# Attention keys and queries projected with a head's columns on the partitions, the rotary embedding made of products and shifted adding transfers

## The chip, the core and the metric

The kernel runs on one core of a Trainium2 chip. The metric is the time of one launch on the device in microseconds (us), the median of several runs. Inputs and outputs lie in device memory (DRAM); the core has a matrix engine (PE, whose weight loads the profile lists as PEld), a vector engine (DVE), a scalar engine (ACT), GpSimd (POOL) and a queue engine (SP). ACT, POOL and SP also issue transfers (DMAs).

## What is computed

One block of a model with two branches, for 256 tokens and 256 context tokens of width 2048, 16 query heads and 4 key/value heads of 128 columns. Both token sets are normalised and modulated, then multiplied by one wide matrix `w_in`; its columns are queries, keys, values and gates of a windowed attention with sinks, five groups of a gated recurrence (HGRN), and two merge gates. Only the part that the change touches is written out:

```python
def apply_axial_rope(x, cos, sin):
    x1, x2, x3, x4 = jnp.split(x, 4, axis=-1)
    rot = jnp.concatenate([-x2, x1, -x4, x3], axis=-1)
    return x * cos[:, None, :] + rot * sin[:, None, :]
q = apply_axial_rope(aq.reshape(B, n, 16, 128), cos, sin) * 128 ** -0.5
k = apply_axial_rope(ak.reshape(B, n, 4, 128), cos, sin)
k_c = cak.reshape(B, L, 4, 128)          # the context's keys are not rotated
out = sink_softmax_av(q @ concat(k_window, k_c).T, concat(v_window, v_c), sink)
```

The rotation adds to each column of a head, times a cosine, the column 32 places away (within its pair of 32-column groups), times a signed sine. The scores need queries and keys with the 128 columns of a head on the partitions and the tokens along the row.

## The kernel before, in words

Every fp32 operand is kept as a high part (rounded to the matrix engine's fp32r) and a low part (the rest). A product is three matmuls: high by high, high by low, low by high. Weights are read from DRAM in pieces of 128x1024 ("chunks", `raw`, five buffers, issued by SP far ahead); ACT rounds a chunk to `wh` (L85) and DVE subtracts it to make `wl` (L86), three buffers each, and PE multiplies.

The stages in order of time:

1. To about 132 us: norms and modulation.
2. To about 440 us: the projections with all 512 tokens and others whose result has tokens on the partitions. `quad_tok` is a Strassen-like product of seven half-size products (L732, L734, L737) with 256 columns each, used for the recurrence's values (four times), for all keys (`C_K`, 512 columns of 4 heads) and for all values (`C_V`); its results go to DRAM (`kv_dr`).
3. From about 440 to 700 us: `quad_col`, the same scheme with a head's columns on the partitions (L660 with 512 columns, L663 with 256), two heads a time, 13 sets, for the forget gates; ACT ends a set with a sigmoid and an affine step and stores it (`F_dr`).
4. From about 700 to 1256 us, the weave: eight pairs of recurrence heads. The small work of a pair (`pair`, a generator) is woven by `weave` with large projections that serve as filler (`side_work`). A filler block is 8 chunks. `proj_tok_g` gives tokens on the partitions (each chunk 12 matmuls of 512 columns: L100, L101, L103); `proj_col_x_g` gives columns on the partitions (each chunk 8 matmuls of 512 columns, L154, high weights by both halves of x, and 8 of 256, L157; two half-blocks of 4 chunks). The blocks are, two per pair: merge, queries 0; merge, gate; queries 1, merge; gates, merge; queries 2, merge; gates, merge; queries 3, merge; the rest. The gates g of the residual are made in the background by `gates`: DVE adds one 128x512 piece of `w_ada` at a time (L204, tile `hgw`), and POOL fetches the next into the same buffer (L541) when DVE is done.
5. Then attention (`attend`) with the output projections as filler, and the two last projections.

In the weave PE's order is written out by the program; DVE, ACT and POOL are ordered by a scheduler that simulates the program, and each engine runs its list strictly in that order. `behind_chunk` only forbids an instruction a place ahead of the last chunk's ACT and DVE steps.

Keys and queries before: at the end of a query block DVE rotates the two 128x512 results from the matmul banks (`rope`, four instructions, L1074 to L1082), ACT stores them (`qr_dr`, L527), and each store puts a task on a list. `tasks_on` starts tasks at fixed places of a pair (filler steps 7, 11, 15): POOL fetches the tile back (L1133), PE turns it with four transposes (`turn_tile`, L1098), ACT and DVE split it into high and low parts (L1100, L1101), and POOL stores those (`q_dr`, L1139). The four key tasks at the weave's start do the same from `kv_dr` (L1106); the tokens' keys are rotated after the fetch.

## Time and profile before

| | |
|---|---|
| median of 3 runs | 1584.49 us (1583.45 to 1588.19) |
| the profiled execution | 1586.59 us, span of its instructions 1584.8 us (1.8 us lie around it) |
| busy share of the span | PE 99%, PEld 85%, DVE 76%, ACT 54%, POOL 9% |
| granted PE clock | 0.999 |
| DMA | 333.83 MB, mean 211 GB/s |
| transfers on POOL's queue | 64.08 MB, 11.8% of 16 engines' span |

A busy PE means only that some matmul is in flight: matmuls overlap, one of 512 columns lasts about 390 ns but a new one starts every 227 to 230 ns. What a group of matmuls costs is therefore read from starts, in the order of time, not from durations. Idle time of an engine off the path costs nothing; a wait on ACT or DVE counts when it makes the next `wh` or `wl` late for PE.

### The profile page before, as it was taken

The numbers are of one execution on the slowest core, as the hardware profiler recorded it, in microseconds if no ns is written. First come the engines' busy times: TensorE is split into PE (matmuls) and PEld (weight loads), VectorE is DVE, ScalarE is ACT, GpSimd is POOL, SyncE is SP. The second block draws the span as 40 slices with busy tenths as digits, with TensorE's granted clock in tenths as the row PEclk, the third lists the DMA queues.
The fourth block names the chain that finished last, engine by engine and source line by source line (L and its number), as shares of the span: only waits on it lengthen the run. The fifth ranks groups of instructions, "written<-read, shape, count | busy, mean of one in ns | idle before, by whom it ended". The sixth has DMA issues, their size and how long they took to land. (4 is left out here: it accounts for less than half of the span.)

```text
span 1584.8 us, 27868 instructions
## 1 busy us (share of the span) xinstructions
PE 1561.6 (99%) x10954; PEld 1343.8 (85%) x10954; DVE 1201.5 (76%) x1764; ACT 860.5 (54%) x1344; POOL 142.1 (9%) x280
## 2 busy tenths in 40 slices
PE   7999999999999999999999999999999999999998
PEld 4568899999988888888888888888888888888887
DVE  4449977777787878878888897888878777757764
ACT  4336443333355555566656666575666776744442
POOL 2000000000000000011212222121121000000000
PEclk9999999999999999999999999999999999999999
DMA  9996734434444444467777877878677854458661
GB/s 366 386 387 230 226 111 130 134 132 134 133 147 127 134 130 137 136 225 252 243 247 244 300 260 233 270 243 273 221 261 249 289 159 154 155 180 295 226 197 69
DMA packets 242900, 333.83 MB, mean 211 GB/s; under 512 B 12080, under 2 KB 162000, under 8 KB 242000
## 3 DMA queue, kind: packets, MB, share of 16 engines
q1 hardware_dynamic: 214096, 249.54, 48.5%
q0 software_dynamic: 19168, 64.08, 11.8%
q10 hardware_dynamic: 9504, 18.42, 3.2%
q8 instruction: 86, 1.41, 0.4%
q14 instruction: 46, 0.38, 0.1%
HBM read 300.53 MB, written 31.47 MB: 209 GB/s over the span
## 5 line engine op out<-in xcount | busy, mean ns | idle before, releaser
L85 ACT ACTIVATE wh<-raw 128x1024 fp32r<-128x1024 f32 x284 | 298.8, 1059 | 236.3 <-PE pj L101 151.7
L86 DVE TENSOR_TENSOR wl<-raw,wh 128x1024 fp32r<-128x1024 f32 x284 | 344.0, 1219 | 89.9 <-ACT wh L85 88.9
L100 PE MATMUL pj<-wh,xHL 128*128 128x512 f32 (+1 forms) x768 | 298.6, 390 | 0.0
L101 PE MATMUL pj<-wh,xHL 128*128 128x512 f32 (+1 forms) x768 | 294.8, 385 | 0.0
L103 PE MATMUL pj<-wl,xHL 128*128 128x512 f32 (+1 forms) x768 | 202.7, 385 | 0.0
L635 ACT ACTIVATE wh<-T 128x1024 fp32r<-128x1024 f32 x75 | 79.5, 1060 | 166.8 <-DVE T L616 83.9
L100 PEld LDWEIGHTS pj<-wh,xHL 128*128 128x128 f32 x768 | 144.4, 188 | 28.2 <-ACT sg L219 0.6
L101 PEld LDWEIGHTS pj<-wh,xHL 128*128 128x128 f32 x768 | 144.5, 188 | 27.6
L103 PEld LDWEIGHTS pj<-wl,xHL 128*128 128x128 f32 x768 | 142.0, 188 | 28.9
L635 ACT ACTIVATE wh<-raw 128x1024 fp32r<-128x1024 f32 x100 | 105.3, 1055 | 71.9 <-PE pj L734 23.7
L154 PE MATMUL pj<-xHL,wh 128*128 128x512 f32 x512 | 130.3, 396 | 0.0
L636 DVE TENSOR_TENSOR wl<-raw,wh 128x1024 fp32r<-128x1024 f32 x100 | 121.8, 1218 | 9.8 <-ACT wh L635 9.7
L636 DVE TENSOR_TENSOR wl<-T,wh 128x1024 fp32r<-128x1024 f32 x75 | 91.5, 1220 | 32.8 <-ACT wh L635 32.8
L154 PEld LDWEIGHTS pj<-xHL,wh 128*128 128x128 f32 x512 | 92.4, 189 | 16.9
L157 PEld LDWEIGHTS pj<-xHL,wl 128*128 128x128 f32 x512 | 69.8, 190 | 5.2
L204 DVE SCALAR_TENSOR_TENSOR acc<-hgw,cg,acc 128x512 f32<-128x512 f32 x60 | 44.9, 748 | 35.0 <-DMA hgw<-in_w_ada_dram 35.0
L157 PE MATMUL pj<-xHL,wl 128*128 128x256 f32 x512 | 71.3, 282 | 0.0
L912 DVE TENSOR_TENSOR A<-A,X 128x512 f32<-128x512 f32 x96 | 61.6, 682 | 0.1
L616 DVE TENSOR_TENSOR T<-raw,T 128x1024 f32<-128x1024 f32 x50 | 60.9, 1218 | 0.1
L616 DVE TENSOR_TENSOR raw<-raw 128x1024 f32<-128x1024 f32 x25 | 30.6, 1225 | 36.7 <-DMA raw<-in_w_in_dram 36.7
L541 POOL DMA_DIRECT2D hgw<-in_w_ada_dram x64 | 35.0, 547 | 235.3 <-DVE acc L204 157.6
L660 PE MATMUL pj<-S,wh 128*128 128x512 f32 x208 | 52.6, 395 | 1.6 <-ACT s L667 1.6
(353 smaller groups left out, 3155.1 us busy)
## 6 DMA issues: line engine op xcount, KB each, us to landing
raw<-in_w_in_dram SPq DMA_DIRECT2D x300, 512.0 KB, 4.6
raw<-in_w_ada_dram SPq DMA_DIRECT2D x64, 512.0 KB, 8.0
hgw<-in_w_ada_dram POOLq DMA_DIRECT2D x64, 256.0 KB, 4.5
raw<-in_w_o_hgrn_dram SPq DMA_DIRECT2D x32, 512.0 KB, 3.6
raw<-in_w_o_attn_dram SPq DMA_DIRECT2D x32, 512.0 KB, 4.1
raw<-in_w_out_dram SPq DMA_DIRECT2D x28, 512.0 KB, 4.1
F<-F POOLq DMA_DIRECT2D x16, 512.0 KB, 7.2
F<-F ACTq DMA_DIRECT2D x13, 512.0 KB, 4.4
```

The costliest lines, as they stand in the source:

```text
L85: last_hi[0] = act.activation(h[:, :n], raw[:, :n], AF.Copy).ins
L86: last_lo[0] = dve.tensor_tensor(lo[:, :n], raw[:, :n], h[:, :n].bitcast(F32), op=ALU.subtract).ins
L100: pe.matmul(o, s[0], m[0], start=first, stop=False)
L101: pe.matmul(o, s[1], m[0], start=False, stop=False)
L103: pe.matmul(o, s[0], m[1], start=False, stop=last)
L154: pe.matmul(o.rearrange("p (a t) -> p a t", a=2), h[:, j, cs_], xHL[:, :, k0 + j, :T], start=k0 + j == 0, stop=False)
L157: pe.matmul(o[:, :T], lo[:, j, cs_], xH[:, k0 + j, :T], start=False, stop=k0 + j == KT - 1)
L616: dve.tensor_tensor(o, x_, y_, op=ALU.subtract)
L635: act.activation(h, src, AF.Copy)
L636: dve.tensor_tensor(lo, src, h.bitcast(F32), op=ALU.subtract)
L660: pe.matmul(m_[z].rearrange("p (z a t) -> p z a t", z=2, a=2), h[:, k, :], mv(k), start=fresh and k == 0, stop=False, skip_group_check=True)
L912: dve.tensor_tensor(av, av, f.unsqueeze(3).to_broadcast([P, 2, n2, b]), op=ALU.mult)
```

## The change

The tables of cosine and sine are turned (columns of a head on the partitions, sines moved by 32 partitions). Keys leave `quad_tok` and become two more sets of `quad_col` (`key_set`), after the first and the third forget set of stage 3; their end is four DVE products of 128x256, two ACT copies and two stores. Queries become `proj_col_x_g` blocks; a half-block ends with two ACT copies and two DVE sums (`halves_into`), two DVE products of 128x512 (`times_row`, by cosine and by sine), and two stores into separate DRAM tiles. A task now fetches the cosine product into `qx` (L1119 after the change), then adds the sine product to it by four accumulating POOL transfers of 32 partitions each, every one from the neighbouring 32 rows (L1125), and then splits with ACT and DVE (L1104, L1105 for keys, L1156, L1157 for queries). No transposes are left on this way. The context's keys are fetched and split with nothing added. `tasks_on` now does one step at a time, at filler steps 5, 7, 9, 11, 13 and 15. The layout of the loaded queries in `attend` follows.

```diff
-    kv_dr = [[dram.tile([P, 1024], F32, name=f"kv{i}_{t}") for t in range(2)] for i in range(2)]
-    qr_dr = [dram.tile([P, 1024], F32, name=f"qr{j}") for j in range(4)]
+    av_dr = [dram.tile([P, 1024], F32, name=f"av{t}") for t in range(2)]
+    k_dr = [[dram.tile([P, w], F32, name=f"k{n}_{w}") for w in (1024, 512)] for n in range(2)]
+    qr_dr = [[dram.tile([P, 1024], F32, name=f"qr{j}_{y}") for y in range(2)] for j in range(4)]
+    def times_row(o, a, c0):
+        dve.tensor_tensor(o.rearrange("p (h t) -> p h t", h=2), a.rearrange("p (h t) -> p h t", h=2),
+                          cs[:, c0: c0 + T].unsqueeze(1).to_broadcast([P, 2, T]), op=ALU.mult)
+    def halves_into(o, bank_):
+        act.activation(o, bank_[:, T:], AF.Copy)
+        dve.tensor_tensor(o, bank_[:, :T], o, op=ALU.add)
+        def key_set(n):
+            def finish(sg):
+                kc = fp.tile([P, 2, 512], F32, tag="F0", name="kc", bufs=2)
+                ks = base.tile([P, 512], F32, tag="bb", name="ks", bufs=2)
+                for i in (1, 0):
+                    for o, c0 in ((kc[:, i, :T], K_COS), (ks[:, i * T: (i + 1) * T], K_SIN)):
+                        dve.tensor_tensor(o, sg[i][:, :T], cs[:, c0: c0 + T], op=ALU.mult)
+                    act.activation(kc[:, i, T:], sg[i][:, T:], AF.Copy)
+                nc.scalar.dma_start(k_dr[n][0], kc.rearrange("p i t -> p (i t)"))
+                nc.scalar.dma_start(k_dr[n][1], ks)
+            quad_col(C_K + 2 * n * HD, finish)
-            for i, co in enumerate((C_K, C_V)):
-                quad_tok(co, kv_dr[i])
+            quad_tok(C_V, av_dr)
             for n in range(1, 8):
...
+                if n < 3:
+                    key_set(n - 1)
-        task[0] = (task[0]() if task[0] else None) or (tasks.pop(0)() if tasks else None)
+        if task[0]:
+            task[0] = task[0]()
+        elif tasks:
+            task[0] = tasks.pop(0)()
+    def rotated(src, then):
+        def fetch():
+            a = base.tile([P, 512], F32, tag="sm", name="qx", bufs=3).rearrange("p (h t) -> p h t", h=2)
+            nc.gpsimd.dma_start(a, src[0])
+            if src[1] is None:
+                return lambda: lambda: then(a)
+            def more():
+                for b in range(4):
+                    nc.gpsimd.dma_start(a[32 * b: 32 * b + 32], src[1][32 * (b ^ 1): 32 * (b ^ 1) + 32], accum_op=ALU.add)
+                return lambda: then(a)
+            return more
+        return fetch
-        bq = yield from proj_tok_g(w_in, C_Q + 512 * j, x_st, range(2))
-        for t in range(2):
-            qr = base.tile([P, 512], F32, tag="sm", name="qr", bufs=3)
-            rope(qr.rearrange("p (r h d) -> p r h d", r=2, h=2), bq[t], t)
-            outs.append((qr_dr[j][:, t * 512: (t + 1) * 512], qr, lambda t=t: fetch(t)))
+        for hf in range(2):
+            cols_ = proj_col_x_g(w_in, C_Q + 512 * j + 256 * hf)
...
+            for i, b in enumerate(bq):
+                halves_into(qs[:, i * T: (i + 1) * T], b)
+            for o, c0 in ((qc, K_COS), (qs, K_SIN)):
+                times_row(o, qs, c0)
...
+            outs.append((dr[0], qc))
+            outs.append((dr[1], qs, rotated([d.rearrange("p (h t) -> p h t", h=2) for d in dr], stored(hf))))
-            if i in (7, 11, 15):
+            if i in (5, 7, 9, 11, 13, 15):
                 tasks_on()
```

How the instructions move is shown at the third query block (queries 2, in the fifth pair), where a task's data are made just before the task.

PE before: two filler chunks in a row with a turn between them; `tkt` is the bank that takes the turned queries, `qr` the tile fetched back:

```order
L101 MATMUL pj<-wh,xHL 128x512
L103 MATMUL pj<-wl,xHL 128x512 x4
L1098 MATMUL tkt<-cs,qr 128x128 x4
L100 MATMUL pj<-wh,xHL 128x512
...
L866 MATMUL al<-Kmt 32x32 x16
```

After the change PE's list has no such row anywhere: L100 follows L103 directly.

POOL before, at the same place: `bb` is a bias for a merge block, `hgw` the fetch for the background gates, `qr` the fetched query tile, `q_0` and `q_1` the high and low part of the result:

```order
L764 DMA bb<-in_b_merge_dram 128x512
L541 DMA hgw<-in_w_ada_dram 128x512
L1133 DMA qr<-qr_133 128x512
L783 MEMSET e 128x1 x2
...
L787 MEMSET e 128x1 x2
L1139 DMA q_0_139<-xHL 128x2x256
L1170 DMA F_10810<-F_6_97 128x1024
L1139 DMA q_1_140<-xHL 128x2x256
```

POOL after, the same place, with the four adding transfers (L1125) between the fetch (L1119) and the next `hgw`:

```order
L1119 DMA qx<-qr_0_137 128x512
L1201 DMA F_10271<-F_5_104 128x1024
L1125 DMA qx<-qr_1_138 32x512 x4
L550 DMA hgw<-in_w_ada_dram 128x512
L794 DMA bb<-in_b_merge_dram 128x512
L1159 DMA q_0_145<-xHL 128x2x256
...
L1159 DMA q_1_146<-xHL 128x2x256
```

The fetch has moved ahead of `bb`, and `hgw`, `bb` and the stores of the result stand behind the adding transfers.

ACT before, from the first of the block's two stores (L527) to the split (L1100):

```order
L527 DMA qr_133<-qr 128x512
L85 ACTIVATE wh<-raw 128x1024
...
L839 ACTIVATE F_9273<-A 128x256 x4
L85 ACTIVATE wh<-raw 128x1024 x2
L842 ACTIVATE acc<-A 128x512
L842 ACTIVATE so<-A 128x512
...
L1100 ACTIVATE xHL<-tkt 128x2x256
```

ACT after, from the first half-block's end (L536) over its stores (L528) and its split (L1156, which reads `qx`) to the second half-block's split (a second row L1156, not repeated, where the last ... stands):

```order
L536 ACTIVATE qr<-pj 128x256 x2
L978 ACTIVATE so<-sb 128x512
...
L528 DMA qr_1_138<-qr 128x512
L85 ACTIVATE wh<-raw 128x1024
...
L1156 ACTIVATE xHL<-qx 128x2x256
L869 ACTIVATE F_9251<-A 128x256 x4
...
L872 ACTIVATE so<-A 128x512
L85 ACTIVATE wh<-raw 128x1024 x4
...
L903 ACTIVATE X_9855<-al 64x4x64 x2
```

Between a half-block's second store and its split stand three chunks' `wh` (four at the second half-block). The first split stands behind the 120th `wh` of line 85 and ahead of the 121st; before, the block's first store stood behind the 121st. The second half's stores stand behind the first half's split, which they did not before, when both tiles were stored together.

More of the change, by code (lines that the diff above doesn't have):

```diff
@@ L1090, in tasks_on, with attn_keys, done, then @@
     def tasks_on():
[L1093 to L1112 removed]
+        if task[0]:
[3 more added lines that the diff above has]
+    def rotated(src, then):
+        def fetch():
+            a = base.tile([P, 512], F32, tag="sm", name="qx", bufs=3).rearrange("p (h t) -> p h t", h=2)
[8 more added lines that the diff above has]
+        return fetch
+    def attn_keys(n):
+        def done(z):
+            def then(a):
                 with behind_chunk():
[L1114 to L1117 removed]
+                    split(*[X[:, 4 * n + z: 4 * n + 4: 2, :] for X in (XH, XL)], a)
+            return then
+        kx, ks = [k_dr[n][y].rearrange("p (h t) -> p h t", h=2) for y in range(2)]
+        return rotated((kx[:, :, :T], ks), done(0)), rotated((kx[:, :, T:], None), done(1))
     def attn_values():
@@ L1179, in side_work @@
         values, NB = attn_values(), 17
-        tasks.extend(attn_keys(z, t) for z in range(2) for t in range(2))
+        tasks.extend(f for n in range(2) for f in attn_keys(n))
         blocks = (merge_out(0, 0), attn_queries(0), merge_out(0, 1), output_gate(3),
@@ L1519, in _constants @@
     cos, sin = np.cos(ang), np.sin(ang) * sign
-    for t in range(2):
-        cst[:, K_COS + t * HD: K_COS + (t + 1) * HD] = cos[t * P: (t + 1) * P]
-        cst[:, K_SIN + t * HD: K_SIN + (t + 1) * HD] = sin[t * P: (t + 1) * P]
+    cst[:, K_COS: K_COS + T] = cos.T
+    cst[:, K_SIN: K_SIN + T] = sin.T[np.arange(HD) ^ 32]
     i, j = np.arange(P)[:, None], np.arange(P)[None, :]
```

78 lines of the change are left out of this document (29 added, 49 removed).

## The prediction

> **What bounds the kernel now.** The order of reading was: the page's busy shares, the stages in windows, the waits, then the engines' instructions in order of time at the places that the change touches. The page's first part, and one row for each of three stages (start:end, length, then busy time and count of PE, PEld, DVE, ACT, POOL, granted clock, DMA share, GB/s):
>
> ```profile
> PE 1561.6 (99%) x10954; PEld 1343.8 (85%) x10954; DVE 1201.5 (76%) x1764; ACT 860.5 (54%) x1344; POOL 142.1 (9%) x280
> ...
> 398.00:440.00 42.00, 42.00 (x352) 42.00 (x351) 31.12 (x30) 15.58 (x16) 1.60 (x3) 1.00 0.44 139
> 440.00:700.00 260.00, 257.69 (x1469) 226.07 (x1468) 206.95 (x233) 150.68 (x194) 5.75 (x14) 1.00 0.46 138
> 700.00:1256.00 556.00, 554.08 (x4906) 475.13 (x4905) 466.00 (x765) 349.93 (x632) 108.23 (x207) 1.00 0.78 259
> ```
>
> PE is idle for 1.9 us of the 556 us weave and for 2.3 us of the 260 us before it. So a microsecond taken off PE's list is a microsecond of the span, and a change elsewhere counts only if it makes PE wait. The waits (engine, line, what it waited for, total, times, longest) say why PE does not wait today:
>
> ```profile
> ACT wh L85 <- PE pj L101: 151.7, 111, 3.1
> ...
> DVE acc L204 <- DMA hgw<-in_w_ada_dram: 35.0, 31, 3.0
> ...
> ACT xHL L1087 <- DMA vr<-kv: 6.1, 1, 6.1
> ...
> PE tkt L1098 <- DMA qr<-qr: 1.0, 2, 0.6
> ```
>
> ACT usually waits for PE to give a chunk buffer back, that is, it runs ahead as far as three buffers allow. That lead is the cover that every late transfer eats into. The one wait of PE on a transfer in the weave is at the turned queries, which the change removes.
>
> **The change part by part.** *Turns.* PE in order of time (start, duration): a turn without a wait, then the two with one.
>
> ```profile
> 750.69 1.07 PE L103 MATMUL pj<-wl,xHL 128*128 128x512 f32 x4
> 751.60 0.60 PE L1098 MATMUL tkt<-cs,kx 128*128 128x128 f32 x4
> 751.96 0.48 PE L100 MATMUL pj<-wh,xHL 128*128 128x512 f32 x1
> 752.27 0.40 PE L101 MATMUL pj<-wh,xHL 128*128 128x512 f32 x1
> ```
> ```profile
> 1010.84 1.07 PE L103 MATMUL pj<-wl,xHL 128*128 128x512 f32 x4
> ...
> 1011.74 0.39 PE L100 MATMUL pj<-wh,xHL 128*128 128x512 f32 x1
> ...
> 1016.28 1.07 PE L103 MATMUL pj<-wl,xHL 128*128 128x512 f32 x4
> 1017.75 0.63 PE L1098 MATMUL tkt<-cs,qr 128*128 128x128 f32 x4 [0.41 <-DMA qr<-qr]
> 1018.14 0.48 PE L100 MATMUL pj<-wh,xHL 128*128 128x512 f32 x1
> ```
> ```profile
> 1149.00 1.07 PE L103 MATMUL pj<-wl,xHL 128*128 128x512 f32 x4
> 1150.70 0.63 PE L1098 MATMUL tkt<-cs,qr 128*128 128x128 f32 x4 [0.63 <-DMA qr<-qr]
> 1151.08 0.47 PE L100 MATMUL pj<-wh,xHL 128*128 128x512 f32 x1
> ```
>
> From L103's start to the next L100 a chunk border costs 0.90 us (1010.84 to 1011.74); with a turn it is 1.27 (750.69 to 751.96), and the matmul behind it starts its successor after 0.31 instead of 0.23. A turn costs 0.37 + 0.08, taken as 0.44; twelve (four key tiles, eight query tiles) make 5.3 us. The two late ones last 1.86 and 2.08, so 0.6 + 0.8 = 1.4 us of waiting goes with them. Removed: 6.7 us.
>
> *Queries on PE.* A `proj_tok_g` chunk takes 2.72 us (1010.84 to 1016.28 is two). A `proj_col_x_g` chunk, from the chain of waits, two chunks apart:
>
> ```profile
> 922.07 1.85 PE pj L154 x8
> ...
> 927.66 1.84 PE pj L154 x8
> ```
>
> That is 5.59 / 2 = 2.795 us, 0.075 more, although both stream 6144 columns. Four blocks of 8 chunks: 32 x 0.075 = +2.4 us, wholly on PE's path. The reason is in the spacings: 2.72/12 = 0.227 us for 512 columns, and for 256, in the window 398 to 440 that holds only such matmuls, 42.00/352 = 0.119, more than half.
>
> The Trainium skill, "TensorE: Matmul & The Clock Gate", Back-to-back issue gap, gives a stream of matmuls N/2.4 + 2.5 ns each, so 215.8 ns for 512 columns and 109.2 for 256; by it the query blocks would be dearer by an estimated 0.3 us only, and the sum 2.1 us lower. This trace disagrees with both figures (227 and 119 ns), and it decides.
>
> *Keys on PE.* A `quad_tok` has 336 matmuls of 256 columns at 0.119: 40.1 us. The window 440 to 700 holds 13 sets of 112 and 13 matmuls of the next projection (about 2.3 us): 257.7 / 13 = 19.8 us a set, its waits included, two make 39.6. Gain 0.5 us. The sets' new end loads DVE with four products of half width, but takes two long ACT steps away; DVE is busy for 207 of 260 us there, so I count nothing (if DVE fell behind at both sets, it would be the four products' time, under 2 us).
>
> *DVE and ACT in the weave.* Rows (shape, count | busy, mean ns):
>
> ```profile
> L839 ACT ACTIVATE F<-A 128x256 f32<-128x256 f32 x64 | 24.2, 441 | 4.6 <-DVE A L912 4.6
> ...
> L165 DVE TENSOR_TENSOR hsum<-pj,hsum 128x256 f32<-128x256 f32 x32 | 12.1, 415 | 0.2 <-ACT hsum L164 0.2
> ...
> L164 ACT ACTIVATE hsum<-pj 128x256 f32<-128x256 f32 x32 | 10.5, 372 | 2.0 <-DMA qr<-qr 1.7 <-DMA hg<-sgg 0.2
> ...
> L1100 ACT ACTIVATE xHL<-tkt 128x512 fp32r<-128x512 f32 x12 | 7.1, 592 | 2.6 <-PE tkt L1098 2.6
> ...
> L1074 DVE TENSOR_TENSOR qr<-pj,cs 128x512 f32<-128x512 f32 x8 | 5.5, 682 | 0.8 <-PE pj L103 0.8
> ```
>
> A rotation was 2 x 0.68 + 2 x 0.41 = 2.2 us of DVE; a half-block's end is 2 x 0.415 + 2 x 0.68 = 2.2 as well, and the splits stay. ACT gets 16 x 0.37 = 6 us more over 556 us in which it is busy for 350. Amounts change nothing; places may.
>
> *The new chain.* POOL is strictly in order. Behind the four adding transfers stand the next `hgw` fetch (for which DVE waits at L204, and DVE makes `wl`), `bb` and the result's stores. And ACT's split now waits for fetch and additions, with `wh` behind it on ACT. At queries 0 and 1 and the keys the products lie in DRAM long before; their tasks need a fetch and an addition only, and I count them as covered. At queries 2 and 3 the store is made just before. Rows for queries 2: the chain of waits for the matmuls that would end the first half-block and those that end the block, then ACT, POOL and landing times.
>
> ```profile
> 985.95 0.92 PE pj L103 x4
> ...
> 1000.12 0.91 PE pj L103 x4
> ```
> ```profile
> 1002.93 1.06 ACT L85 ACTIVATE wh<-raw 128x1024 fp32r<-128x1024 f32 x1 [0.60 <-ACT wh L85]
> ...
> 1005.65 1.06 ACT L85 ACTIVATE wh<-raw 128x1024 fp32r<-128x1024 f32 x1 [0.62 <-ACT qk L842]
> 1006.56 0.33 ACTq L527 DMA_DIRECT2D qr<-qr  x1
> ```
> ```profile
> 1011.11 0.54 POOL L1133 DMA_DIRECT2D qr<-qr  x1 [1.96 <-DMA qr<-qr]
> ```
> ```profile
> F<-F POOLq DMA_DIRECT2D x16, 512.0 KB, 7.2
> ...
> v<-v POOLq DMA_DIRECT2D x32, 128.0 KB, 4.8
> q<-xHL POOLq DMA_DIRECT2D x16, 256.0 KB, 6.4
> ...
> hgw<-hg POOLq DMA_DIRECT2D x8, 256.0 KB, 3.1
> ```
>
> Before: block end 1001.0, store 1006.6 (5.6 later), landed 1011.1 (4.5), fetched back by 1017.7 (6.6; the turn's wait ends there). After, first half: end 986.9, store 5.6 later (992.5), landed 997.0, fetched 1003.6, four issues of 0.54 each (the last begins at 1005.2), landing. No row shows an adding transfer. Its landing lies between 3.1 and 7.2 us, the ends of POOL's own rows; I take 4.8, the row with the smallest transfers: 1010.0. ACT reaches the split behind its 120th `wh`, at 1004.0 (1002.93 + 1.06), and waits 6 us. The 121st `wh` then ends at 1013.4 (split 0.59, four copies of L839 1.76, `wh` 1.06) instead of 1006.7; PE wanted it at 1011.7. So 0 to 1.7 us of PE waiting. ACT's split of the values (L1087, above) waited 6.1 us for its fetch, and PE lists no wait for it: I take 0 for the first half. The second half:
>
> ```profile
> 1020.27 1.06 ACT L85 ACTIVATE wh<-raw 128x1024 fp32r<-128x1024 f32 x1 [0.83 <-PE pj L101]
> ...
> 1028.64 2.53 ACT L888 ACTIVATE X<-X 32x128 f32<-32x128 f32 x8
> ```
> ```profile
> 1032.16 2.09 PE L154 MATMUL pj<-xHL,wh 128*128 128x512 f32 x8
> ```
>
> The second half's stores stand behind that split and another `wh`, so at about 1013: landed 1017.5, fetched 1024.1, last issue 1025.7, landed 1030.5. ACT is there at 1021.3 (1020.27 + 1.06) and waits 9 us; split, the eight copies of L888 and `wh` (0.6 + 2.5 + 1.1) end at 1034.7, when PE wanted the chunk at 1032.2. That is 2.5 us, with the smaller copies beside them 2.6. Queries 3 stand alike, so 5.2 us return.
>
> Sum: -5.3 - 1.4 + 2.4 - 0.5 + 5.2 = +0.4 us. On the profiled 1586.59 us: 1587.0. That execution lies 2.1 above the median of 1584.49, and on the median's scale the forecast is 1584.9.
>
> **The rivals.** *1, the lead covers the chain.* For it speaks the `vr` wait that cost nothing; against it that 9 us is longer than 6. Nothing returns: -4.8 us, 1579.7.
>
> *2, the additions are late (the other side).* At 6.4 us (the row of `q`) every chain is 1.6 longer: first halves 1.7 + 1.6, second halves 2.6 + 1.6, twice: 15.0 us return, and -4.8 + 15.0 = +10.2 on the median is 1594.7. It decides from a return of 9.6 us on, that is with first halves uncovered (8.6) and a landing of 5.0. For it: `hgw`'s DVE wait, 35.0 us already, grows with it; four transfers want the same engines at a DMA share of 0.78. Against it: they are small. The Trainium skill, "DMA: Bandwidth & Descriptors", Rules for kernel authors, says that transfers to disjoint partition ranges serialise and that one over all partitions is better, which speaks against this change: at that page's 2.0 us + bytes/436 GB/s, four of 64 KB in a row would take an estimated 8.6 us, 3.8 more than I take, so a return of 8.6 + 4 x 3.8 = 23.8 and an estimated 1603.5; no run here shows it yet.
>
> *3, half-width matmuls cost exactly half.* If 256 columns took 0.1135 us, queries and keys would cost what they did, and with rival 1's cover -6.7 remains: 1577.8. The 0.119 speaks against it.
>
> **How the numbers follow.** A difference of 0.3% (4.75 us) is about what a measurement of this kernel tells from no change; "same" is 1579.7 to 1589.2. Forecast: 0.40. Rival 1: 0.30; its time lies at the border, and 0.19 of it I count as faster. Rival 2: 0.27. Rival 3: 0.03. Faster: 0.19 + 0.03 = 0.22. Slower: 0.27 + 0.06 for a forecast with the first halves uncovered: 0.33. Same: the rest, 0.45. The range goes from between rivals 3 and 1 (1579.0) to rival 2 (1595.5). Faster and slower weigh alike enough that the forecast's own range stands beside it: 1582.3 (half the return) to 1588.5 (first halves uncovered).
>
> **What would show it.** No L1098; L154 with 768 instead of 512 instances at an unchanged spacing; 15 sets at 19.8 us. The landing of `qx` on POOL from 32 rows: 4.8 says forecast, over 5.0 rival 2. ACT's waits at L1156 near 1004 and 1021, and PE idle behind `wh` there and 133 us later. I am wrong if PE's idle time in the weave stays under 2 us, if it grows at queries 0 or 1 or the keys, or if stages that I left out move.

## The result, and the profile after the change

The kernel after the change takes 1605.96 us (median of 4 runs, 1603.67 to 1608.65) against 1585.36 us before in the same series: a ratio of 1.0128, 95% interval 1.011 to 1.0146. It is 20.6 us slower; the forecast was +0.4, and the range ended at 1595.5. The profiled execution, the longest of the four, took 1608.65 us with a span of 1606.9.

The profile's first part and the two stages (same columns as before):

```profile
PE 1567.5 (98%) x10922; PEld 1346.2 (84%) x10922; DVE 1203.1 (75%) x1771; ACT 865.4 (54%) x1370; POOL 174.6 (11%) x318
...
440.00:700.00 260.00, 259.21 (x1478) 227.45 (x1477) 210.97 (x241) 151.02 (x196) 5.23 (x13) 1.00 0.47 143
700.00:1256.00 556.00, 536.05 (x4839) 460.42 (x4838) 446.40 (x730) 335.47 (x619) 138.32 (x241) 0.99 0.78 254
```

The stage with the two new key sets is as full as it was. In the weave PE is idle for 20.0 us of the 556 where it was idle for 1.9, and the granted clock is 0.99. So the whole loss lies there. How long the weave is can be read from two matmuls that every version has, the first `tw` (the first pair's start) and the first `sc` (attention's start); "a to b" is the first and the last start. Before, then after:

```profile
L929 PE MATMUL tw<-cs,F x64: 272/273/300, 709.1 to 1174.2; 128*128 128x128 f32 x64
L92 PE MATMUL sc<-xHL,qTa x32: 389/476/481, 1247.3 to 1390.1; 128*128 128x512 f32 x32
```
```profile
L959 PE MATMUL tw<-cs,F x64: 272/273/327, 706.7 to 1194.0; 128*128 128x128 f32 x64
L92 PE MATMUL sc<-xHL,qTa x32: 389/476/481, 1269.2 to 1412.0; 128*128 128x512 f32 x32
```

538.2 us have become 562.5: +24.3. All that comes before is 2.4 us shorter. This length is a measure below; it is from one execution each, and spans of one kernel differ by a few microseconds (1600.7 to 1606.9 in the four runs of this one). Where a conclusion hangs on less than that, the medians of the times stand beside it.

The waits after the change that answer to those shown before:

```profile
ACT xHL L1156 <- DMA qx<-qr: 39.1, 8, 9.7
DVE acc L204 <- DMA hgw<-in_w_ada_dram: 38.3, 24, 3.4
...
POOL qx L1125 <- DMA qx<-qr: 26.3, 8, 5.9
...
ACT Kmt L872 <- DVE A L942: 19.6, 7, 6.3
...
ACT X L908 <- DVE X L911: 17.5, 8, 6.8
...
PE pj L154 <- ACT wh L85: 8.2, 5, 2.3
```

All eight query splits wait for their additions, queries 0 and 1 too. ACT also waits longer for DVE (L872, L908); the rows for the same two instructions before the change were

```profile
ACT X L878 <- DVE X L881: 16.2, 7, 5.1
...
ACT Kmt L842 <- DVE A L912: 10.6, 7, 3.5
```

And PE now waits for `wh`. Three places show the kinds of wait.

**The additions.** Queries 1, first half: POOL, then ACT, then PE.

```profile
929.87 0.54 POOL L1119 DMA_DIRECT2D qx<-qr  x1
935.52 3.21 POOL L1125 DMA_DIRECT2D qx<-qr  x4 [5.11 <-DMA qx<-qr]
```
```profile
943.82 0.63 ACT L1156 ACTIVATE xHL<-qx 128x512 fp32r<-128x512 f32 x1 [7.79 <-DMA qx<-qr]
```
```profile
946.49 0.50 PE L100 MATMUL pj<-wh,xHL 128*128 128x512 f32 x1 [2.31 <-ACT wh L85]
...
947.76 0.61 PE L101 MATMUL pj<-wh,xHL 128*128 128x512 f32 x1
948.16 0.63 PE L100 MATMUL pj<-wh,xHL 128*128 128x512 f32 x1
948.59 0.63 PE L101 MATMUL pj<-wh,xHL 128*128 128x512 f32 x1
```

From the fetch to the split it is 14 us, of which 8.3 from the first addition on. ACT came 7.8 us early, its lead is gone, PE stands for 2.3 us. And a moment after the stall matmuls start every 0.43 us in place of 0.23: PE runs at half its rate for a while.

**A gate step inside the pair's chain.** DVE, ACT and PE 30 us later, and DVE and ACT at the same place before the change:

```profile
967.45 0.30 DVE L911 COPY_PREDICATED X<-mk,al 128x128 f32<-128x128 uint8 x1
970.65 0.75 DVE L204 SCALAR_TENSOR_TENSOR acc<-hgw,cg,acc 128x512 f32<-128x512 f32 x1 [2.91 <-DMA hgw<-in_w_ada_dram]
971.32 0.30 DVE L911 COPY_PREDICATED X<-mk,al 128x128 f32<-128x128 uint8 x1
```
```profile
971.65 0.28 ACT L908 ACTIVATE X<-al 128x128 f32<-128x128 f32 x1 [6.78 <-DVE X L911]
```
```profile
975.49 2.11 PE L154 MATMUL pj<-xHL,wh 128*128 128x512 f32 x8 [2.25 <-ACT wh L85]
```
```profile
953.72 0.75 DVE L204 SCALAR_TENSOR_TENSOR acc<-hgw,cg,acc 128x512 f32<-128x512 f32 x1 [0.29 <-DMA hgw<-in_w_ada_dram]
...
957.26 0.63 DVE L881 COPY_PREDICATED X<-mk,al 128x128 f32<-128x128 uint8 x2
```
```profile
957.99 0.28 ACT L878 ACTIVATE X<-al 128x128 f32<-128x128 f32 x1 [3.15 <-DVE X L881]
```

Before, the gate's step stood ahead of the pair's two masked copies. Now the scheduler has put it between them. It waits 2.9 us for its `hgw` fetch, the second copy and so ACT wait with it, and the next `wh` is 2.3 us late.

**A key task on POOL.** POOL, and PE:

```profile
778.59 3.23 POOL L1125 DMA_DIRECT2D qx<-k  x4 [2.46 <-DMA qx<-k]
781.90 0.47 POOL L191 TENSOR_SCALAR ss<-ss 128x4 f32<-128x4 f32 x1
```
```profile
784.50 1.42 PE L1054 MATMUL to<-cs,so 128*128 128x128 f32 x4 [3.30 <-DVE so L1046]
```

POOL waits for the key's fetch, issues the four additions, and only then does a small product `ss` for the pair (before, it began at 778.42 without a wait). PE stands for 3.3 us.

### The profile page after: what moved, and what is told of

Read it like the earlier page. It is cut to its first block, busy times and chain, and to the rows that moved or that the text cites. A ratio compares the mean times of both kernels' runs of the same rounds, so it can differ in the third digit from the quotient of the medians.

```text
span 1606.9 us, 27906 instructions
## 1 busy us (share of the span) xinstructions
PE 1567.5 (98%) x10922; PEld 1346.2 (84%) x10922; DVE 1203.1 (75%) x1771; ACT 865.4 (54%) x1370; POOL 174.6 (11%) x318
## 5 line engine op out<-in xcount | busy, mean ns | idle before, releaser
L100 PE MATMUL pj<-wh,xHL 128*128 128x512 f32 (+1 forms) x640 | 248.5, 390 | 3.3 <-ACT wh L85 3.3
L101 PE MATMUL pj<-wh,xHL 128*128 128x512 f32 (+1 forms) x640 | 246.4, 387 | 1.6 <-issue 1.6
L154 PE MATMUL pj<-xHL,wh 128*128 128x512 f32 x768 | 197.1, 398 | 8.2 <-ACT wh L85 8.2
L103 PE MATMUL pj<-wl,xHL 128*128 128x512 f32 (+1 forms) x640 | 170.3, 388 | 1.5 <-DVE wl L86 1.5
L154 PEld LDWEIGHTS pj<-xHL,wh 128*128 128x128 f32 x768 | 138.9, 189 | 34.8 <-ACT wh L85 9.1
L100 PEld LDWEIGHTS pj<-wh,xHL 128*128 128x128 f32 x640 | 121.2, 189 | 29.9 <-ACT wh L85 4.4
L101 PEld LDWEIGHTS pj<-wh,xHL 128*128 128x128 f32 x640 | 121.2, 189 | 23.8 <-issue 0.6
L103 PEld LDWEIGHTS pj<-wl,xHL 128*128 128x128 f32 x640 | 118.9, 190 | 26.5 <-DVE wl L86 2.6
L157 PEld LDWEIGHTS pj<-xHL,wl 128*128 128x128 f32 x768 | 105.1, 191 | 8.2 <-DVE wl L86 0.5
L157 PE MATMUL pj<-xHL,wl 128*128 128x256 f32 x768 | 107.5, 283 | 0.0
L204 DVE SCALAR_TENSOR_TENSOR acc<-hgw,cg,acc 128x512 f32<-128x512 f32 x60 | 44.8, 747 | 38.3 <-DMA hgw<-in_w_ada_dram 38.3
L550 POOL DMA_DIRECT2D hgw<-in_w_ada_dram x64 | 44.3, 691 | 202.1 <-DVE acc L204 151.9
L668 PE MATMUL pm<-S,wh 128*128 128x512 f32 x256 | 64.6, 394 | 0.3 <-ACT s L675 0.3
```

Source lines behind the costliest of these rows:

```text
L100: pe.matmul(o, s[0], m[0], start=first, stop=False)
L101: pe.matmul(o, s[1], m[0], start=False, stop=False)
L103: pe.matmul(o, s[0], m[1], start=False, stop=last)
L154: pe.matmul(o.rearrange("p (a t) -> p a t", a=2), h[:, j, cs_], xHL[:, :, k0 + j, :T], start=k0 + j == 0, stop=False)
L157: pe.matmul(o[:, :T], lo[:, j, cs_], xH[:, k0 + j, :T], start=False, stop=k0 + j == KT - 1)
L668: pe.matmul(m_[z].rearrange("p (z a t) -> p z a t", z=2, a=2), h[:, k, :], mv(k), start=fresh and k == 0, stop=False, skip_group_check=True)
```

## The experiments

Length of the weave, from `tw` to `sc` as above (the profiled execution), and the ratio of the medians to that of the kernel before in the same series:

| run | weave, us | ratio, 95% interval |
|---|---|---|
| before | 538.2 | |
| after | 562.5 | 1.0128, 1.0110 to 1.0146 |
| 1 keys only, new places | 554.9 | 1.0108, 1.0089 to 1.0127 |
| 2 queries only | 559.3 | 1.0140, 1.0122 to 1.0158 |
| 3 no additions | 546.3 | 1.0062, 1.0043 to 1.0082 |
| 4 split a step later | 556.7 | 1.0135, 1.0105 to 1.0165 |
| 5 before, no gates | 536.3 | 1.0067, 1.0052 to 1.0082 |
| 6 after, no gates | 544.4 | 1.0124, 1.0109 to 1.0139 |
| 7 shift by DVE | 562.5 | 1.0138, 1.0123 to 1.0154 |
| 8 keys only, old places | 537.6 | 1.0001, 0.9991 to 1.0012 |
| 9 additions from SBUF | 549.4 | 1.0054, 1.0038 to 1.0069 |
| 10 fetch on ACT's queue | 566.4 | 1.0135, 1.0100 to 1.0170 |
| 11 shift by ACT | 544.7 | 1.0038, 1.0022 to 1.0053 |
| 12 split later and pinned | 557.6 | 1.0090, 1.0058 to 1.0123 |
| 13 no additions, no gates | 529.8 | 1.0024, 1.0015 to 1.0034 |
| 14 projection only | 543.5 | 1.0036, 1.0021 to 1.0051 |
| 15 steps 3 apart | 550.9 | 1.0073, 1.0058 to 1.0088 |
| 16 shift by ACT, old places | 546.0 | 1.0051, 1.0034 to 1.0069 |
| 17 before, gates shifted | 543.5 | 1.0036, 1.0022 to 1.0049 |
| 18 after, gates shifted | 563.1 | 1.0155, 1.0128 to 1.0181 |

Runs 5, 6 and 13 leave out the gates' background sums, and their first stage became longer, for a reason that was not looked for (100 to 120 us: 351 GB/s where the kernel before moves 388). They are therefore compared among themselves, and by the weave.

Runs 9, 11, 12, 15 and 16 also hold the split of a query task under `behind_chunk`, which the changed kernel does not do; runs 7, 9, 11 and 16 keep both products in the three buffers of `sm`. In runs 1, 2 and 8 the old rotation reads the turned tables, so that its numbers differ and its work is as before.

**Runs 1 and 2, the change in halves.** Run 1 takes queries from the kernel before, run 2 keys.

```diff
# run 1
-        for hf in range(2):
-            cols_ = proj_col_x_g(w_in, C_Q + 512 * j + 256 * hf)
+        bq = yield from proj_tok_g(w_in, C_Q + 512 * j, x_st, range(2))
# run 2
+            quad_tok(C_K, kw_dr)
-                if n < 3:
-                    key_set(n - 1)
```

> Keys as after the change, queries as before (tokens on the partitions, old rotation, turns by PE; the old rotation reads the turned table, so only its numbers differ). Theory, late additions: in the trace after the change PE loses 3.5 us ahead of L1054 at 781 and 2.5 us more at half clock behind it, because POOL's small product for that row stands behind the four adding transfers of a key task. Four turns (1.8 us) and 0.5 us of the key projection go, so about +4 on the time before: 1587 to 1592. Rival, more transfers in all delay everything: keys make 2 of the 10 additions and a fifth of the loss, +4 as well, but spread, with no single stall over 2 us. The time alone does not tell the two apart; the place of the stall does.

> Queries as after the change, keys as before. Theory, late additions: the eight query tasks keep their stalls (about 19 us with the half-clock stretches behind them), less 3.6 us of turns and 1.4 of waits, plus 2.4 of the dearer projection: about +16, 1598 to 1604. Rival, more transfers in all: nearly the same time, so this run only says how the loss divides between keys and queries.

Measured: 1603.93 and 1607.96 us. Each half alone seems to cost nearly the whole. But in run 1 the loss has a place of its own, the old turns:

```profile
PE tkt L1167 <- DMA qr<-qr: 14.7, 3, 7.1
```

PE waits at turns for the tile fetched back, since run 1 has the new, closer places of the tasks' steps (two filler steps apart in place of four). So run 1 says nothing of the keys; it shows that a step follows its fetch too closely.

**Run 3, the additions left out.**

```diff
-                for b in range(4):
-                    nc.gpsimd.dma_start(a[32 * b: 32 * b + 32], src[1][32 * (b ^ 1): 32 * (b ^ 1) + 32], accum_op=ALU.add)
```

> The adding transfers are left out, everything else is as after the change: the sine product is stored but never added, so the rotation is incomplete. Theory, late additions: ACT's waits at its splits (39 us after the change) fall below 12, PE's stalls and the half-clock stretches go, and the time falls to 1579 to 1584. Rival, it is the chain of store and fetch and the extra 5 MB of transfers: only the additions' share of the bytes goes, and the time stays above 1592.

Measured: 1596.66 us, between the two. By the medians 9.3 of the 20.6 us go with the additions and 11.3 stay; by the weave 16.2 go and 8.1 stay, but the profiled execution, 1592.51 us, was the shortest of its four. ACT's waits at the splits fall from 39.1 to 18.4 us. So late additions are a cause, and not the only one.

**Run 4, more time for the additions.**

```diff
-                return lambda: then(a)
+                return lambda: (lambda: then(a))
             return more
```

> One empty step stands between the additions and the split, so the split and all that follows of a task come about two filler steps later; nothing is left out and no transfer is saved. Theory, late additions: what costs is only that ACT and DVE reach the split before the additions have landed; with some 5 us more in hand ACT's waits there go below 10 us in all and the time falls to 1580 to 1588 (the upper end if POOL's stall at a key task stays). Rival, the transfers themselves load the queues: the time stays above 1598.

Measured: 1606.07 us; ACT still waits 38.1 us at the splits. A step more in the program gave no time on the chip: in its trace the fetch of queries 2's first half is issued at 1064.1, behind an `hgw` fetch and two others, and ACT stands at the split from 1069.9 on. So ACT reaches the split 6 us after the fetch is issued, too soon for fetch and additions.

**Runs 5 and 6, no background gates.** `gates` only ends with its last step; its fetches and sums are gone.

```diff
-        fetch(0, 0)
-        yield
-        for g in range(4):
-            for k0 in range(KT):
-                gate_chunk(accT[:, 0, :], g, k0)
...
+        yield
```

> The kernel before without the background gates: their fetches and DVE's sums are left out (the residual's gates stay at their start values). Control for the next run. DVE loses 45 us of work and its 35 us of waits at L204; PE lost nothing to them, and loses only 16 transposes (about 1.8 us): 1581 to 1585 under either theory.

> The kernel after the change without the background gates, to be read against the kernel before without them (not against the kernel before). First theory, now in two parts: late additions hold ACT (about 14 us of the 25 lost), and a new order on DVE puts a gate step that waits for its fetch ahead of a result that ACT waits for (about 7 us: the stalls at 973 and 1021 to 1025). Then the second part goes and the difference between the two kernels falls from 21 to 10 to 16 us. Rival, additions alone: the difference stays at 18 or more. Rival, the order on DVE alone: it falls below 5.

Measured: 1598.03 and 1606.98 us. The first is 13 us above the expected range, by its first stage alone (the first `tw` stands at 722.8 in place of 709.1); its weave is 1.9 us shorter than before, about what the transposes were expected to take. The difference between the two is 8.9 us (weaves: 8.1), where it was 20.6 (24.3). So the gates are a part too, of about 12 us by the medians and 16 by the weaves, more than expected, and neither rival holds. They do not act through the additions: ACT's waits at the splits stay at 37.7 us in run 6. Its two waits for DVE in the weave (the rows L872 and L908 above) fall from 37.1 us together to 16.7.

**Run 13, neither additions nor gates** (the edits of runs 3 and 6 together).

> After the change without the additions (as in the run without them) and without the background gates; to be read against the kernel before without gates, 1598.0. Each of the two alone took the extra length of the weave from 24 us to 8. Theory, additions and gates share POOL's queue and DVE's list and are the whole of the loss: with both gone the kernel is 2 to 4 us shorter than its control, which is the saved PE work: 1593 to 1597. Rival, the queries' projection in half-blocks or the splits without a turn cost by themselves: the 8 us stay: 1602 to 1608.

Measured: 1592.06 us, 6.0 below its control (1598.03). The weave in one row: PE is never idle. Below it the rows by which its length is read, for run 13 and for its control, run 5:

```profile
700.00:1256.00 556.00, 556.00 (x5020) 483.59 (x5019) 425.42 (x689) 355.43 (x648) 74.48 (x152) 1.00 0.73 236
```
```profile
L950 PE MATMUL tw<-cs,F x64: 272/273/273, 723.4 to 1181.8; 128*128 128x128 f32 x64
L92 PE MATMUL sc<-xHL,qTa x32: 389/474/476, 1253.2 to 1395.9; 128*128 128x512 f32 x32
```
```profile
L920 PE MATMUL tw<-cs,F x64: 272/273/273, 722.8 to 1187.2; 128*128 128x128 f32 x64
L92 PE MATMUL sc<-xHL,qTa x32: 389/474/476, 1259.1 to 1401.8; 128*128 128x512 f32 x32
```

The weave is 529.8 us against 536.3: 6.5 us shorter. The four cases together:

| weave of the changed kernel less that of the kernel before | with gates | without gates |
|---|---|---|
| with additions | +24.3 (medians +20.6) | +8.1 (+8.9) |
| without additions | +8.1 (+11.3) | -6.5 (-6.0) |

This says what the loss is made of. By the weaves additions cost 16.2 or 14.6 us and gates the same. By the medians additions cost 9.3 or 14.9, gates 11.7 or 17.3, the larger figure where the other is left out; the even split by the weaves comes from which executions were profiled. Either way each of the two costs about 9 to 17 us, and under both lies the saving.

**Runs 7 and 11, no transfers for the queries.** The shift by 32 partitions is made inside the core, by DVE writing its sine products to other partitions, or by four ACT copies.

```diff
# run 11 (run 7: four DVE products of 32x512 into qt)
+            for b in range(4):
+                act.activation(qt[32 * b: 32 * b + 32], qs[32 * (b ^ 1): 32 * (b ^ 1) + 32], AF.Copy)
+            dve.tensor_tensor(qc, qc, qt, op=ALU.add)
```

> Queries without any transfer: DVE writes the sine products straight to the neighbouring 32 partitions (four products of 32x512 in place of one of 128x512), adds them, and a task only splits and stores. Nothing is left out; keys stay as after the change, with their additions. DVE gets about 3 us more per half-block. First theory in two parts: all waits for the queries' additions go (about 14 us), the keys' 6 us and part of the 7 us of DVE's order stay: 1587 to 1594. Rival, the order on DVE alone: DVE is busier, the loss stays: over 1600. If keys cost nothing either, below 1583.

> As the run in which DVE writes shifted products, but DVE makes one full sine product and ACT moves it to the neighbouring partitions by four copies of 32x512; no transfers, nothing left out. There DVE was late by 3 us at each of three query pairs. If DVE's extra 2 us a half-block were the cause, as both theories say of that run, the time falls to 1585 to 1597; if the products' place in DVE's order is, whatever their number, it stays above 1600.

Measured: 1608.80 and 1594.01 us. Run 7 has no waits for additions at queries and is no faster than the change; PE's waits are now for DVE:

```profile
PE kt L1002 <- DVE A L942: 9.4, 4, 3.1
```

With the copies on ACT the loss falls by 15 us. So DVE seems to have no room for 2 us more per half-block, and ACT has; but run 11 also pins the split, and the pin's share (from run 4 to run 12 the excess fell from 20.7 to 15.2 us) was not measured apart.

**Run 8, keys only, old places.** As run 1, with the query tasks' steps at 7, 11 and 15 from the third pair on.

```diff
-            if i in (5, 7, 9, 11, 13, 15):
-                tasks_on()
+            if n < 2:
+                if i in (5, 7, 9, 11, 13, 15):
+                    tasks_on()
+            elif i in (7, 11, 15):
+                task[0] = (task[0]() if task[0] else None) or (tasks.pop(0)() if tasks else None)
```

> Keys as after the change, queries as before, as in the first run; but the query tasks now have the old places too (filler steps 7, 11 and 15 from the third pair on). In the first run PE stood 2.0, 5.9 and 7.3 us ahead of turns, which only says that a turn two steps behind its fetch comes too early. Under the theory those stalls go and what is left is the keys' own: a wait for POOL near 781, 1.8 us of turns saved: 1584 to 1591. If the loss is in any change of order, it stays above 1595.

Measured: 1587.28 us, ratio 1.0001. The keys' part of the change costs nothing and gains nothing measurable: four turns fewer, against stalls of 1.2 us at `to`, where POOL's `ss` begins at 782.8, right behind the four additions that are issued from 779.5 on.

**Runs 9, 10, 12 and 15, the chain of a query task.** Run 9 adds from SBUF (the core's own memory) at once, without store and fetch; run 10 fetches on ACT's queue; run 12 is run 4 with the split under `behind_chunk`; run 15 puts the steps three apart.

```diff
# run 9
+                for b in range(4):
+                    nc.gpsimd.dma_start(qc[32 * b: 32 * b + 32], qs[32 * (b ^ 1): 32 * (b ^ 1) + 32], accum_op=ALU.add)
# run 10
-            nc.gpsimd.dma_start(a, src[0])
+            with behind_chunk():
+                nc.scalar.dma_start(a, src[0])
# run 15
-            if i in (5, 7, 9, 11, 13, 15):
+            elif i in (3, 6, 9, 12, 15):
```

> The rotation's sum without DRAM: at the place where the two products were stored, four accumulating POOL transfers add the sine product from SBUF straight to the cosine product, each shifted by 32 partitions; no store, no fetch, and a task only splits and stores the result, one empty step later and pinned behind the last chunk's steps. Nothing is left out. New theory, POOL's queue: what was late was POOL, which in order waits for the background gates' fetch buffers, then for its own fetch to land, and only then issues the additions, so that the split is early whatever step it stands at. One hop in place of three then brings ACT's waits at the splits under 10 us and the time to 1583 to 1593. Rival, DVE's order (the gates' steps between results that ACT waits for) alone: over 1598.

> One line is changed: a task's fetch is issued on ACT's queue, pinned behind the last chunk's steps, in place of POOL's; the additions stay on POOL. Theory, POOL's queue: the fetch starts when ACT gets there, ahead of POOL, POOL waits less than the 26 us for its landing, and about half of the loss goes: 1588 to 1600. Rival, DVE's order alone: no change, 1602 to 1609.

> The run with an empty step between additions and split, with the query's split pinned behind the last chunk's ACT and DVE steps, as the keys' split is (whose waits were 0). Theory, POOL's queue: the fetch and the additions lag by what POOL waits for, so the pin gains only where the split had been moved ahead of its step (queries 1 and 2, second halves): 1594 to 1603. Rival, the split stands too early because nothing holds it at its step: waits under 10 us, 1583 to 1592.

> After the change with the query tasks' steps three filler steps apart in place of two (from the third pair on; a step that ends a task also begins the next, as before the change), the split pinned. Nothing is left out. Theory, the chain of fetch, additions and split needs 13 to 15 us and two steps of two chunks each give it 11, from which POOL's lag is taken: with 17 us ACT's waits at the splits fall from 39 to under 20 us and the time to 1588 to 1600. Rival, the distance does not matter since POOL lags by more: 1602 to 1609.

Measured: 1598.43, 1611.41, 1603.21 and 1600.16 us. ACT's waits at the splits, one row from each, in this order:

```profile
ACT xHL L1161 <- DMA qr<-qr: 3.8, 3, 1.5
```
```profile
ACT xHL L1157 <- DMA qx<-qr: 42.1, 7, 10.2
```
```profile
ACT xHL L1157 <- DMA qx<-qr: 33.5, 6, 8.6
```
```profile
ACT xHL L1157 <- DMA qx<-qr: 10.4, 3, 5.3
```

Where the waits go (runs 9 and 15), 12 to 13 us of the weave go, and 11 to 13 stay above the kernel before (8 to 10 and 10 to 13 by the medians). After run 4 I thought that POOL's place for the fetch was the reason. Run 10 gives that no support, and does not refute it: on ACT's queue the waits are as long, but the fetches hardly start earlier (six of the eight by 0.2 to 3.8 us, at queries 1 at 927.4 in place of 929.9, and two by 3 us later). What helps is a shorter chain or more distance.

**Runs 14 and 16.** Run 14 stores the sums of the halves as they are: rotation, tasks and splits of the queries are left out. It makes each sum twice (its trace has 32 copies L536 and 32 sums L537 where the changed kernel has 16), so 0.75 us of ACT and 0.83 of DVE per half-block take the place of the rotation's 1.37 on DVE. Run 16 is run 11 with one store, one fetch and the old places.

```diff
# run 14
-            for o, c0 in ((qc, K_COS), (qs, K_SIN)):
-                times_row(o, qs, c0)
+            for y in range(2):
+                outs.append((q_dr[j][y][:, hf * 512: (hf + 1) * 512], qs))
```

> Queries as after the change up to the sums of the two halves, which are stored as they are; rotation, tasks and splits of the queries are left out, keys are as after. Theory, the loss is in what comes behind the projection: PE loses nothing to it and keeps the saving of turns: 1579 to 1586. Rival, eight half-block ends with ACT copies and DVE sums in the middle of a block disturb the pair's work: over 1590.

> The version that the runs point to: rotation inside the core (DVE's two products, four shifting ACT copies, one DVE sum), one store, and a task of two steps as before the change (fetch, then split) at the old places, filler steps 7, 11 and 15, from the third pair on; the split pinned. No additions by transfer for queries; nothing is left out. Theory: PE keeps the saving (about 3 us net) and ACT and DVE are no later than before: 1580 to 1588. Rival, DVE's extra sum and ACT's extra copies are late for the pair's chain: 1591 to 1600.

Measured: 1592.84 and 1595.75 us, both above their expectation. Even with only the second sums and the stores behind the projection the weave is 5.3 us longer than before (medians 5.5). Two places where PE stands, with 3.3 and 3.6 us, come to more than that. One is of the key task's kind:

```profile
PE to L1054 <- DVE so L1046: 3.3, 2, 3.1
```

The other stands at the end of the background gates, where PE turns their finished column (L564):

```profile
1223.10 0.27 PE L564 MATMUL tgr<-cs,gcol 128*16 128x128 f32 x1 [2.31 <-DVE gcol L214]
...
1226.69 0.50 PE L100 MATMUL pj<-wh,xHL 128*128 128x512 f32 x1 [1.29 <-ACT grow L566]
```

DVE makes that column behind a split of the values, which waits for its fetch. The changed kernel loses 1.4 and 1.4 us at this place, the kernel before 0.4.

No version tried is faster than the kernel before.

**Runs 17 and 18, the gates' places alone.** The counter that starts a gate step begins at half its threshold.

```diff
-        gate, count = gates(), [0]
+        gate, count = gates(), [0.575 * STEP]
```

> The kernel before with the background gates' steps half a period earlier: the counter that starts a gate step begins at half its threshold, nothing else. The gates cost 1.9 us of the weave's length in the kernel before and 16 to 18 after the change. Theory, that is a matter of where in DVE's list a gate step falls (between two results that ACT waits for, or beside them): the old kernel's places happened to be harmless, and with others it loses 4 to 15 us: 1589 to 1600. Rival, the old order takes any phase and only the change's own instructions make gate steps harmful: 1583 to 1588.

> The kernel after the change with the same shift of the gates' phase. Theory, a matter of places: the weave's length moves by several microseconds either way, 1594 to 1612, while ACT's waits for the additions stay (30 to 45 us). Rival, the change's own instructions: 1603 to 1609, as after the change.

Measured: 1593.23 and 1611.78 us. In the kernel before, whose work is untouched, other places for the gates' steps cost 5.3 us of the weave (medians 5.6): its order was a good one. In the kernel after they change its length by 0.6 us (medians 3.6 more over the kernel before, with intervals that overlap). So places matter, but a bad phase alone does not explain what the gates cost the changed kernel.

## Why the prediction was wrong

*PE's own work: right in the main.* Turns, their waits, the dearer projection and the keys summed to -4.8 us; without additions and gates the median is 6.0 us below its control. The terms were not measured one by one, but a chunk of the dearer projection still takes 2.79 us (starts at 988.14 and 990.93 after the change), which leaves nothing of rival 3. The first `tw` comes 2.4 us earlier than before in the profiled pair; over all profiled runs with the new key sets and with gates it stands at 708.0 on average, over those with the old keys at 709.0, so about 1 us where 0.5 was forecast. The section of the Trainium skill that the prediction names for the spacing of matmuls gives its formula for an isolated one, not for a stream; the sum did not use it.

*The landing of an addition: right, and so, nearly, its chain.* I took 4.8 us:

```profile
qx<-qr POOLq DMA_DIRECT2D x32, 64.0 KB, 4.9
```

The split has to wait for the last of four. From the first issue to the last landing the eight query tasks took 5.1 to 9.4 us, 7.7 on average, where 1.6 + 4.8 = 6.4 was forecast; from the fetch's issue to the split they took 10.4 to 15.5, 13.7 on average, where 6.6 + 6.4 = 13.0 was. The Trainium skill, "DMA: Bandwidth & Descriptors", Rules for kernel authors, has transfers to disjoint partition ranges serialise, an estimated 8.6 us for four of 64 KB by that page's formula. The four at queries 1, landed 8.1 us after the first issue, come near that sum, but this trace does not show them one behind the other: each is under way for about 6 us, and they land within 2.0 us of each other, since POOL issues them about 0.5 us apart (L1125 between 935 and 938):

```profile
DMA to landing us min/median/max: 5.8/6.1/6.5
```

The prediction's 1603.5 set those 8.6 us, which count from the first issue, against 4.8, which count from the last; against 6.4 they are 2.2 more, a return of 8.6 + 4 x 2.2 = 17.4 and 1597.1. With the measured 1.3 more it is 13.8 and 1593.5. So longer additions at queries 2 and 3 do not make the measured time.

*The step that failed first: "At queries 0 and 1 and the keys the products lie in DRAM long before; their tasks need a fetch and an addition only, and I count them as covered."* ACT waited at all eight query splits, 7.8 us at queries 1, where PE then stood for 2.3; the prediction had named idle time there as a sign of being wrong. That the data are old is no cover. The chain runs from the task's own fetch, 14 us, while its steps are two filler steps of 2.8 us apart, 11 us in all, and ACT stood at the splits 5.4 to 12.1 us after the fetch was issued: it gets there ahead of PE, by the lead that I had counted as cover for the wait. The keys were covered at their splits, but not on POOL, where a small product stood behind their additions, and PE stood for 3.3 us. Leaving the additions out took 9 to 16 us off.

*The step that failed second: "Amounts change nothing; places may."* I priced places at nothing. The gates cost 1.9 us of the weave before and 12 to 17 after, as much as the additions. Their fetch is no later than it was (4.7 us to landing, 4.5 before), and their own waits are as long (38.3 us, 35.0 before); what grew is ACT's waiting for DVE behind them. The same two waits (L872 and L908 after the change, L842 and L878 before) were together 26.8 us before, 37.1 after, and 49.4 in run 3, without additions; without gates they are 8.8 before (run 5), 16.7 after (run 6) and 20.3 without additions (run 13).

*A term that was missing: the clock.* A stall costs more than its length (below): 5, 3 and 2.5 us at half rate lose half of that, an estimated 5 of the 24.3 us; 18.1 are PE's additional idle time.

*The rivals.* Rival 2 had the right side and half of the mechanism, late additions and DVE's wait for `hgw`; its price of 10.2 us was short of the measured 20.6 because it too had queries 0 and 1 and the keys covered. The sizes of single stalls were good: 2.6 us forecast for queries 2's second half, where PE then stood for 1.9 us and ACT for 5.9. Rival 1's lead was shorter than 6 us: there, ACT's 5.9 cost PE 1.9. Nor was the `vr` wait of 6.1 us, which spoke for it, free before the change: DVE's column for the finished gates stood behind it, and PE waited 0.4 us for that (at 1220.9); after the change the same wait of 6.1 us stands ahead of the 1.4 and 1.4.

*What stays open.* That the gates are about half of the loss is shown by leaving them out, which takes away their DVE sums, their fetches on POOL and 16 transposes at once. That it is the place of the DVE sums, and not the fetches' place on POOL, is argued from ACT's waits for DVE and from places like the one at 971; two phases of the gates gave nearly the same length, and no run put them elsewhere one at a time.

## What to carry to other kernels

When a step on the bound engine is taken out, look at what it held in place: here the split stood behind a turn on PE, and without it ACT came too early for transfers that take 14 us (no run put the turn back alone). In a kernel whose bound engine is never idle, price every new in-order wait with everything queued behind it on that engine, and treat old data as uncovered until the fetch itself is. And test an order by shifting it: a tuned kernel stands on places that any edit moves, and a shift of the gates alone cost the kernel before 5 us.

## What the runs showed of the hardware that was not expected

PE's clock fell after some short stalls. Windows of 20 us after the change, with the granted clock after POOL's busy time:

```profile
780.00:800.00 20.00, 16.66 (x71) 13.43 (x70) 15.49 (x29) 10.93 (x17) 6.42 (x10) 0.83 0.60 188
...
940.00:960.00 20.00, 17.68 (x71) 14.11 (x70) 14.43 (x23) 13.29 (x23) 7.44 (x14) 0.91 0.76 230
960.00:980.00 20.00, 17.75 (x219) 15.14 (x219) 13.62 (x19) 10.45 (x20) 2.40 (x4) 1.00 0.83 273
1040.00:1060.00 20.00, 18.07 (x111) 16.15 (x110) 14.69 (x24) 15.09 (x37) 6.00 (x10) 0.91 0.88 293
```

A stall of 3.3 us (at 784.5) is followed by 5 us at half rate, one of 2.3 us (946.5) by 3 us, one of about 1.9 us (1046) by 2.5 us, and others of 2.25 us (975.5) and 2.3 (1184.9) by none. The Trainium skill, "TensorE: Matmul & The Clock Gate", Part 1: The HAM clock gate, gives half clock after an idle window of about 3.4 us that runs free of the program. The halved spacing and the chance in it agree; that 1.9 us can be enough does not, and the measurement decides.

DVE and ACT read 32 partitions and wrote 32 others in these runs, and it cost what a whole tile does. The shifting copies of run 11 and products of run 7, by shape:

```profile
L1179 ACT ACTIVATE qt<-qr 32x512 f32<-32x512 f32 x32 | 20.2, 630 | 6.1 <-DVE qr L532 5.8
```
```profile
L1178 DVE TENSOR_TENSOR qt<-qr,cs 32x512 f32<-32x512 f32 x32 | 21.9, 683 | 0.4
```

A product of 128x512 took 682 ns before the change (L1074), and ACT's split of 128x512 at 943.82 took 0.63 us: a quarter of the partitions saved nothing.
